# A fixed TensorE order for the recurrence stage of a decoder block, and 64-wide blocks for one level of its triangular inverse

## The chip, the core and the metric

The kernel runs on one core of a Trainium2 chip. A core has a matrix engine (TensorE, PE in the profile, with its weight loads shown apart as PEld), a vector engine (VectorE, DVE), a scalar engine (ScalarE, ACT), GpSimd (POOL) and SyncE (SP), which here issues nearly all transfers. Each engine executes its own instructions in the order in which the program holds them, and waits on semaphores for the others. Matrix products are accumulated in PSUM, which TensorE writes and VectorE and ScalarE read; everything else lies in SBUF or in device memory.

The metric is the time of one execution in microseconds (us); lower is better.

## The reference, cut to what matters

One block of a decoder, one sequence of 512 tokens, model width 2048, all float32:

```python
h = rmsnorm(x) * (1 + sc1) + sh1                 # sh, sc, gt: six parts of silu(c) @ w_ada + b_ada
p = h @ w_in                                     # r, k, v (1024 each), three low-rank inputs, 1024 for pooling
y_rwkv = rwkv7_mixer(...)                        # 16 heads of width 64
y_pool = pool_mixer(...)                         # causal means over windows 2, 4, 8, 16
x = x + gt1 * (concat(y_rwkv, y_pool) @ w_out)
h = rmsnorm(x) * (1 + sc2) + sh2
x = x + gt2 * conv_ffn(h)                        # up-projection, causal conv, silu gate, down-projection
return rmsnorm(x)

# inside rwkv7_mixer, per head, for each token t:
sa = S @ a_t
S  = S * w_t + outer(sa, b_t) + outer(v_t, k_t)
y_t = S @ r_t
```

The mixer is the part at issue. The kernel computes it in chunks of 64 tokens. Inside a chunk the recurrence asks for the inverse of a 64 x 64 unit triangular matrix for each head and chunk; from chunk to chunk a 64 x 64 state is carried on.

## The kernel before

Large products are made in three matmuls: both operands are split into a high part of the type fp32r and a remainder, and `mm3` (lines 122 to 124) adds high x high, high x low and low x high. "A k-tile" below is one such group of three matmuls, 128 x 128 by 128 x 512. The weights of four k-tiles are loaded, rounded on ScalarE (L115, `whi`) and subtracted on VectorE (L117, `wlo`); three buffers of each exist.

The program has these stages in time: the norm and the first eight column blocks of the input projection (tiles `pf`); the recurrence stage, which this change rewrites; the output projection; the feed-forward part.

The recurrence stage has four kinds of work.

- **The rest of the input projection**: 27 column blocks of 16 k-tiles each, 432 k-tiles in all. `win_pair(p)` makes r, k and v of head pair p, shifts them by a token and spills them to device memory; three pool groups of two blocks each follow.
- **Eight head pairs**, each with three functions. `stage_a` makes decays and keys, the scores `bt` against `ar` (L473, tile `pa`), masks them (L414), and inverts the 16 x 16 diagonal blocks: the blocks go to device memory (L419) and come back in another layout (L423); 28 small VectorE instructions (L431 and L433, between L425 and L434) make the inverse; it goes to device memory again (L439), comes back as `x4l` (L442), and ScalarE copies it to `x4` (L445). `stage_b` makes other scores and transposes, and then two levels of products that widen the inverse from 16 to 32 (L512, L521, L524) and from 32 to 64 (L533 to L539). `stage_c` uses the inverse, runs six dependent steps from chunk to chunk (L588 on TensorE, L589 on VectorE), and normalises and gates the result.
- **Pooling** of four groups (`pool_front` on VectorE, `pool_back` on TensorE).
- **`ada_rest`**: 192 rows of a matrix-vector product, each a transfer of 256 KB (L346) and a VectorE instruction with an accumulator read (L347).

The order of the instructions on every engine is made by a scheduler when the program is built. It models the engines' time, takes what is ready, and prefers what has the higher priority. `hp()` gives the pairs' work a higher priority than the projection and `ada_rest`, so the projection's matmuls fill in wherever a pair waits. The granularity is one matmul. Of the input projection, `win_pair(p + 2)` is written ahead of `stage_a(p + 1)`.

`atile` gives one of two PSUM buffers (`pa`), `mmtile` one of two (`mm`), `btile` a double bank (`pb`, and `py` for the outputs).

Of the kernel before, what the change touches and what calls it, by code (L numbers as in the profile page):

```python
# [57 lines left out]
def block_kernel(ctx, tc, a, out, stop=None, dbg=None):  # L58
# [217 lines left out]
    def pool_front(gi):  # L276
# [19 lines left out]
    def pool_back(gi, zs, pw):  # L296
        for d in range(2):
            ps = atile()
            for i in range(2):
                PE.matmul(ps, pw[:, i, d * P : (d + 1) * P], zs[i], start=i == 0, stop=i == 1)  # L300
            j = gi * 2 + d
            mx = ring("mxp")
            S.activation(mx, ps, AF.Identity, bias=drv[:, 35 + j : 36 + j], scale=col("psc", j))
            if gi:
                nc.sync.dma_start(mixd[8 + j], mx)
            else:
                last_mix.append(split_act(14 + d, mx))

# [13 lines left out]
    def win_tile(fi):  # L322
        ps = mmtile()
        project(ps, a["win1"][fi - 8, :, :], H)
        return ps
# [3 lines left out]
    xy = ra.tile([P, 2, 8, 64], F32, tag="xy", name="xy")  # L329
    G.memset(xy, 0.0)  # L330
    dxz = [tc.dram_tile([32, 2, 32, 32], F32, name=f"dxz{i}") for i in range(2)]
    for i in range(2):
        nc.sync.dma_start(dxz[i][:, :, :, :].rearrange("l w i j -> (l w i j)").rearrange("(p n) -> p n", p=P),
                          xy[:, :, :, 0:32])
# [21 lines left out]
    def r8(t, n=64):  # L356
        return t[:, 0 : 8 * n].rearrange("p (s j) -> p s j", s=8)
# [4 lines left out]
    def stage_a(p, rkv):  # L362
        q = Pair()
# [43 lines left out]
        V.tensor_mul(ch(bt), ch(bt), em[:, :, 1 : L + 1])  # L407

# [3 lines left out]
        scores([pss[h] for h in range(2)], bt, ar)  # L412
# [32 lines left out]
        S.copy(q.x4, x4)  # L445


        k2 = ring("k2")
        S.activation(k2, al, AF.Identity, bias=drv[:, 27 + p : 28 + p], scale=col("ka", p))
        V.tensor_mul(k2, k2, k)  # L450
        kt = q.kt = ra.tile([P, T], F32, tag="kt", name="kt", bufs=2)
        V.tensor_mul(ch(kt), ch(k2), em[:, :, 1 : L + 1])
        V.scalar_tensor_tensor(k2, r, col("rk", p), k2, op0=ALU.mult, op1=ALU.mult)
# [5 lines left out]
        return q  # L459

    def half32(b):
        return slice(32 * (b % 2), 32 * (b % 2) + 32)

    def jl(j):
        return slice(j * L, (j + 1) * L)

    def scores(banks, keys, ar):

        for c in range(NC):
            for e in range(2):  # L470
                for h in range(2):
                    j = 2 * c + e
                    PE.matmul(banks[h][HS[e], c * 2 * L : (c + 1) * 2 * L], keys[HS[h], jl(j)], ar[HS[h], :, j, :],  # L473
                              start=True, stop=True)
# [4 lines left out]
    def to_rows(src, dst, eng):  # L479
# [4 lines left out]
        eng(dst, ps[:, :].rearrange("p (c h d) -> p h c d", c=NC, h=2))  # L484

    def stage_b(p, q):
        sb, x4, ar, bt, kt, v = q.sb, q.x4, q.ar, q.bt, q.kt, q.v
        nt = sb[:, :, 0, :]

        tok = q.tok = ra.tile([P, 2, 8, L], F32, tag="tok", name="tok")  # L490
        rw = q.rw = ra.tile([P, 8, 2, L], F32, tag="rw", name="rw")
        sk = q.sk = ra.tile([P, 8, 2, L], F32, tag="sk", name="sk")
# [4 lines left out]
        to_rows(lambda c: v[:, c * P : (c + 1) * P], by_head(tok[:, 0, :, :]), S.copy)  # L497
        to_rows(lambda c: ar[:, 0, 2 * c : 2 * c + 2, :].rearrange("p e t -> p (e t)"), by_head(rw[:, :, 0, :]), S.copy)
        to_rows(lambda c: bt[:, c * P : (c + 1) * P], by_head(sb[:, :, 2, :]), S.copy)
        to_rows(lambda c: kt[:, c * P : (c + 1) * P], by_head(tok[:, 1, :, :]), S.copy)  # L500
        pl = atile()
        for s in range(8):
            for e in range(2):
                PE.matmul(pl[HS[e], jl(s)], sk[HS[e], s, 0, :], tok[HS[e], 0, s, :], start=True, stop=True)
        S.copy(rw[:, :, 1, :], r8(pl))

        X, Y = x4[:, :, 0, :], x4[:, :, 1, :]
        pt = btile()
        pT, pX = pt[:, 0, :], pt[:, 1, :]
        for s in range(8):  # L510
            for b in range(4):
                PE.matmul(pT[BS[b], s * 32 : s * 32 + 32], nt[BS[b], s, half32(b)], X[BS[b], s, :], start=True, stop=True,  # L512
                          tile_position=(32 * b, 32 * b))
        Tm = ra.tile([P, 8, 32], F32, tag="Tm", name="Tm4")
        V.tensor_mul(Tm, r8(pT, 32), mlev[:, 0:1, 0:32].to_broadcast([P, 8, 32]))
        for w in range(2):
# [758 lines left out]
```

## Time and profile before

| | us |
|---|---|
| three executions: median (lowest to highest) | 2380.74 (2366.47 to 2384.72) |
| the profiled execution | 2386.22 |
| its span, first to last instruction | 2384.5 |
| TensorE busy in the span | 2248.9 |
| VectorE busy | 1623.7 |
| ScalarE busy | 1051.7 |
| mean granted TensorE clock, as a share of full speed | 0.973 |

The profiled execution is 1.7 us longer than its span, and 5.5 us longer than the median of the three. "Busy" of TensorE counts pipelined matmuls to modelled ends, so that it is more than the time between their starts. A row of a group gives source line, engine, operation, output and inputs, sizes and count, then the busy time, the mean time of one in ns, and the idle time of the engine ahead of them with what ended it. A row of the timeline gives start and duration in us. A row of a stretch gives its limits, its length, each engine's busy time with the number of instructions, the granted clock, and the share of time in which the transfer engines were busy.

### The profile page before, as it was taken

Reading aid. Unit: us, or ns where it says so; the run is one execution under the profiler, and the core shown is the slowest. Engines: PE = TensorE matmul, PEld = TensorE weight load, DVE = VectorE, ACT = ScalarE, POOL = GpSimd, SP = SyncE. Lnnn points to the kernel's source line nnn. Section 1 sums busy time; section 2 is a strip of 40 time slices with the busy share of each in tenths; the row PEclk is TensorE's granted clock in tenths of the full one; section 3 lists DMA queues with packets and bytes.
Section 4 is the critical chain, followed back from the end, with each engine's and each line's share of the span. In section 5 each row is a group of like instructions: output and inputs, shape, how many; then the busy total and the mean of one; then the engine's idle time right before and its main releaser. Section 6 shows DMA issues by size and latency. Waiting matters only on the chain.

```text
span 2384.5 us, 44692 instructions
## 1 busy us (share of the span) xinstructions
PE 2248.9 (94%) x18114; PEld 1976.6 (83%) x18114; DVE 1623.7 (68%) x2567; ACT 1051.7 (44%) x1451; POOL 126.1 (5%) x183
## 2 busy tenths in 40 slices
PE   4778888999899999999999999999999999999997
PEld 3656666766666789999999999999999888888897
DVE  7987576777774456688888877777777635353354
ACT  3235243444432335655555555555555522233353
POOL 0000000000000000011010100000000000110000
PEclk9999888999989999999999999999999999999999
DMA  9975555556752666498888887777777767763464
GB/s 360 340 228 163 147 162 156 164 168 189 202 168 80 213 203 200 145 293 231 248 234 241 233 220 196 198 197 198 199 198 194 242 206 266 234 203 118 123 185 160
DMA packets 226241, 482.99 MB, mean 203 GB/s; under 512 B 74545, under 2 KB 79729, under 8 KB 217841
## 3 DMA queue, kind: packets, MB, share of 16 engines
q1 hardware_dynamic: 206114, 413.01, 54.5%
q0 software_dynamic: 18864, 66.07, 13.7%
q8 instruction: 142, 2.33, 0.4%
q10 hardware_dynamic: 1056, 1.05, 0.1%
q14 instruction: 65, 0.53, 0.1%
HBM read 441.50 MB, written 38.54 MB: 201 GB/s over the span
## 4 chain that ended last, share of the span: by engine, by line
PE 50%; issue 8%; DVE 1%; ACT 1%; DMA 0%; POOL 0%; POOLq 0%; DVEq 0%; ACTq 0%
PE b L124 17%; PE b L122 17%; PE b L123 17%; ACT x L796 0%; DMA wrow<-wup 0%; DVE xr L793 0%; DVE ulo L865 0%; ACT t L801 0%; DVE t L905 0%; POOL x L1149 0%; DVE wlo L117 0%; DVE u L894 0%; ACT uhi L863 0%; DVE acc L746 0%; POOLq L1270 0%
## 5 line engine op out<-in xcount | busy, mean ns | idle before, releaser
L124 PE MATMUL b<-t,ulo 128*128 128x256 f32 x1408 | 397.2, 282 | 0.0
L122 PE MATMUL b<-t,uhi 128*128 128x256 f32 x1408 | 396.8, 282 | 0.0
L123 PE MATMUL b<-t,uhi 128*128 128x256 f32 x1408 | 396.7, 282 | 0.0
L115 ACT CAST whi<-wraw 128x512 fp32r<-128x512 f32 x236 | 144.9, 618 | 377.5 <-PE mm L123 241.1
L124 PE MATMUL b<-act,ulo 128*128 128x512 f32 (+1 forms) x880 | 308.0, 350 | 0.0
L123 PE MATMUL b<-act,uhi 128*128 128x512 f32 (+1 forms) x880 | 307.7, 350 | 0.0
L122 PE MATMUL b<-act,uhi 128*128 128x512 f32 (+1 forms) x880 | 307.7, 350 | 0.0
L122 PE MATMUL b<-y,uhi 128*128 128x256 f32 x1056 | 298.4, 283 | 2.2 <-ACT uhi L863 2.2
L124 PE MATMUL b<-y,ulo 128*128 128x256 f32 x1056 | 298.0, 282 | 1.0 <-DVE ulo L865 1.0
L123 PE MATMUL b<-y,uhi 128*128 128x256 f32 x1056 | 297.8, 282 | 0.0
L865 DVE TENSOR_TENSOR ulo<-wd,uhi 128x1024 fp32r<-128x1024 f32 (+1 forms) x120 | 136.1, 1135 | 212.0 <-ACT uhi L863 207.2
L122 PEld LDWEIGHTS b<-t,uhi 128*128 128x128 f32 x1408 | 266.9, 190 | 0.0
L124 PEld LDWEIGHTS b<-t,ulo 128*128 128x128 f32 x1408 | 266.9, 190 | 0.0
L123 PEld LDWEIGHTS b<-t,uhi 128*128 128x128 f32 x1408 | 266.8, 190 | 0.0
L863 ACT CAST uhi<-wquart 128x1024 fp32r<-128x1024 f32 x156 | 163.8, 1050 | 203.7 <-PE b L123 174.7
L863 ACT CAST uhi<-wd 128x1024 fp32r<-128x1024 f32 (+1 forms) x120 | 117.3, 978 | 286.8 <-PE b L123 286.7
L865 DVE TENSOR_TENSOR ulo<-wquart,uhi 128x1024 fp32r<-128x1024 f32 x156 | 190.7, 1223 | 72.3 <-ACT uhi L863 71.8
L117 DVE TENSOR_TENSOR wlo<-wraw,whi 128x512 fp32r<-128x512 f32 x236 | 161.0, 687 | 108.6 <-ACT whi L115 100.8
L863 ACT CAST uhi<-r 128x1024 fp32r<-128x1024 f32 x132 | 138.6, 1050 | 163.6 <-PE b L123 163.6
L865 DVE TENSOR_TENSOR ulo<-r,uhi 128x1024 fp32r<-128x1024 f32 x132 | 161.2, 1221 | 62.2 <-ACT uhi L863 62.1
L122 PE MATMUL mm<-ah,whi 128*128 128x512 f32 x464 | 196.9, 424 | 6.2 <-ACT upad L267 5.5
L122 PEld LDWEIGHTS b<-y,uhi 128*128 128x128 f32 x1056 | 200.3, 190 | 2.9 <-ACT uhi L863 2.8
(301 smaller groups left out, 4575.6 us busy)
## 6 DMA issues: line engine op xcount, KB each, us to landing
wquart<-wup SPq DMA_DIRECT2D x176, 512.0 KB, 4.8
wa<-ada SPq DMA_DIRECT2D x48, 1024.0 KB, 6.0
war<-ada SPq DMA_DIRECT2D x192, 256.0 KB, 3.5
wd<-wdn SPq DMA_DIRECT2D x80, 512.0 KB, 4.0
wraw<-win SPq DMA_DIRECT2D x140, 256.0 KB, 4.0
wraw<-wout SPq DMA_DIRECT2D x96, 256.0 KB, 3.4
wquart<-wup POOLq DMA_DIRECT2D x44, 512.0 KB, 7.5
r<-wup SPq DMA_DIRECT2D x44, 512.0 KB, 4.5
```

The costliest lines, as they stand in the source:

```text
L115: S.copy(hi, raw)
L117: eng.tensor_tensor(lo, raw, hi[:, :].bitcast(F32), op=ALU.subtract)
L122: PE.matmul(ps, wh, xh, start=start, stop=False, skip_group_check=more)
L123: PE.matmul(ps, wh, xl, start=False, stop=False, skip_group_check=more)
L124: return PE.matmul(ps, wl, xh, start=False, stop=stop, skip_group_check=more)
L863: S.copy(hi[:, 0:n], src)
L865: lo_of[0] = V.tensor_tensor(lo[:, 0:n], src, hi[:, 0:n].bitcast(F32), op=ALU.subtract)
```

## The change

The order on TensorE is no longer the scheduler's within the recurrence stage: the block `tc.manual_schedule` keeps TensorE's instructions in the order in which the program writes them. The other engines are still ordered by the scheduler. A loop, `recurrence`, writes the work. It holds three chains: `b` (the former `stage_b` and `stage_c` of a pair in one generator), `a` (`stage_a`) and `p` (pooling). Each generator yields two estimates after a step, the TensorE time of the step and the gap until its next step can run, and the loop keeps a clock of its own from them. Where a chain is ready by that clock its next step is written (b ahead of a ahead of p); otherwise one k-tile of the projection, counted as 0.69, and after every second k-tile one row of `ada_rest`. For the inverse, `stage_a` notes a time 27.0 after its scores, and `stage_b` puts its first product with the inverse at that time.

The 16 to 32 level works on 64-wide blocks: `x4` is now 128 x (8, 2, 64) with zeros outside the 32-wide blocks, each product is 16 matmuls of 64 x 64 where it was 32 of 32 x 32, and one VectorE addition replaces four. The copy on ScalarE (now L483) is twice as wide. In `stage_a` the instructions of `k2` and `kt` now stand ahead of the small VectorE instructions. The last products of a pair's outputs stand together after the chunk steps, and the normalisation uses the banks of `py` in place of `pa`. New line numbers: scores L381, mask L447, small instructions L464 to L473, store L478, load L480, first product with the inverse L530, the other products of the two levels L542, L550 and L555, chunk steps L601.

```diff
+    def win_units(fi, ps):
+        src = a["win1"][fi - 8, :, :]
+        for k0 in range(0, KT, WC // P):
+            wh, wl = split_weights(src[:, k0 * P : k0 * P + WC])
+            for kk in range(WC // P):
...
+                mm3(ps, wh[:, sl], wl[:, sl], *H[k], start=k == 0, stop=k == KT - 1)
+                yield
...
-    xy = ra.tile([P, 2, 8, 64], F32, tag="xy", name="xy")
-    G.memset(xy, 0.0)
+    x4w = ra.tile([P, 8, 2, 64], F32, tag="x4", name="x4w")
+    G.memset(x4w, 0.0)
...
@@ stage_a @@
+        sq = ring("sq")
+        S.activation(sq, k, AF.Square, scale=col("kk", p))
+        yield 0.0, 4.0
...
         V.tensor_mul(fdec[:, 0 : NL - 1, :], ep[:, 0 : NL - 1, L : L + 1], em[:, 1:NL, 0:1])
-        sq = ring("sq")
-        S.activation(sq, k, AF.Square, scale=col("kk", p))
+        yield 1.4, 2.0
...
         V.tensor_mul(ch(bt), ch(bt), em[:, :, 1 : L + 1])
+        yield 0.9, 13.0
...
             nc.sync.dma_start(nl[32 * e : 32 * e + 32, :, :], dn[0:32, es, es])
+        k2 = ring("k2")
+        S.activation(k2, al, AF.Identity, bias=drv[:, 27 + p : 28 + p], scale=col("ka", p))
+        V.tensor_mul(k2, k2, k)
+        kt = q.kt = ra.tile([P, T], F32, tag="kt", name="kt", bufs=2)
+        V.tensor_mul(ch(kt), ch(k2), em[:, :, 1 : L + 1])
+        V.scalar_tensor_tensor(k2, r, col("rk", p), k2, op0=ALU.mult, op1=ALU.mult)
...
-        x4 = ra.tile([P, 8, 2, 32], F32, tag="x4", name="x4l")
         for b in range(4):
-            nc.sync.dma_start(x4[BS[b], :, :, :], dx[8 * b : 8 * b + 8, :, :, :].rearrange("s w i j -> i s w j"))
-        q.x4 = ra.tile([P, 8, 2, 32], F32, tag="x4c", name="x4")
-        S.copy(q.x4, x4)
+            nc.sync.dma_start(x4w[BS[b], :, :, half32(b)],
+                              dx[8 * b : 8 * b + 8, :, :, :].rearrange("s w i j -> i s w j"))
+        x4 = q.x4 = ra.tile([P, 8, 2, 64], F32, tag="x4c", name="x4")
+        S.copy(x4, x4w)
+        q.inverted = clock[0] + 27.0
+        yield 1.4, 6.0
...
@@ stage_b @@
+        yield 0.9, max(1.5, q.inverted - clock[0] - 0.9)
...
-        for s in range(8):
-            for b in range(4):
-                PE.matmul(pT[BS[b], s * 32 : s * 32 + 32], nt[BS[b], s, half32(b)], X[BS[b], s, :], start=True, stop=True,
-                          tile_position=(32 * b, 32 * b))
+        for s, e in diag:
+            PE.matmul(pT[HS[e], jl(s)], nt[HS[e], s, :], X[HS[e], s, :], start=True, stop=True)
...
         for w in range(2):
-            for s in range(8):
-                o = 256 * w + s * 32
-                for b in range(4):
-                    l, r_ = (Y, Tm) if w == 0 else (Tm, Y)
-                    PE.matmul(pX[BS[b], o : o + 32], l[BS[b], s, :], r_[BS[b], s, :], start=True, stop=True,
-                              tile_position=(32 * b, 32 * b))
-        for b in range(4):
-            V.tensor_add(xy[BS[b], :, :, half32(b)], x4[BS[b]].rearrange("p s w j -> p w s j"),
-                         pX[BS[b], :].rearrange("p (w s j) -> p w s j", w=2, s=8))
+            for s, e in diag:
+                l, r_ = (Y, Tm) if w == 0 else (Tm, Y)
+                PE.matmul(pX[HS[e], w, jl(s)], l[HS[e], s, :], r_[HS[e], s, :], start=True, stop=True)
+        V.tensor_add(x4, x4, pX[:, :, :].rearrange("p w (s j) -> p s w j", s=8))
+        yield 2.1, 2.3
...
         for j in range(1, NL - 1):
             o = pg[:, j % 2, jl(j // 2)]
             PE.matmul(o, gd[:, j, :], hs[:, j - 1, :], start=True, stop=True)
             V.scalar_tensor_tensor(hs[:, j, :], o, fdec[:, j, :], hs[:, j, :], op0=ALU.mult, op1=ALU.add)
+            yield 0.25, 1.1
...
-        pyc = atile()
+        pyc = py[:, 0, :]
...
-    pool_back(3, pool_front(3), load_pw(3))
-    with hp():
-        q = start_pair(0)
-        stage_b(0, q)
-    win_pair(1)
-    for p in range(NP):
-        if p + 1 < NP:
-            if p + 2 < NP:
-                win_pair(p + 2)
+    def recurrence():
+        units, n, adas = projection(), 0, 0
+        live = {"b": None, "a": None, "p": pool_group(3, load_pw(3), upad)}
+        ready = {"b": 0.0, "a": 0.0, "p": 0.0}
...
+        while True:
+            if live["a"] is None and na < NP and na in made and (na < 2 or hasattr(qs[na - 2], "left")):
+                live["a"], ready["a"] = stage_a(na, qs[na]), clock[0]
+            if live["b"] is None and nb < na:
+                live["b"], ready["b"] = stage_b(nb, qs[nb]), clock[0]
...
+            for c in "bap":
+                if live[c] is not None and ready[c] <= clock[0]:
+                    break
+            else:
+                if more:
+                    more = next(units, 1) is None
+                    if more:
+                        clock[0] += 0.69
+                        n += 1
+                        if n % 2 == 0:
+                            m = min(192, adas + 1)
+                            ada_rest(adas, m)
+                            adas = m
+                    continue
...
             with hp():
-                qn = start_pair(p + 1)
-        with hp():
-            stage_c(p, q)
-            if p + 1 < NP:
-                stage_b(p + 1, qn)
-                q = qn
-        ada_rest(min(28 * p, 192), min(28 * p + 28, 192))
+                step = next(live[c], None)
...
+                clock[0] += step[0]
+                ready[c] = clock[0] + step[1]
+
+    with tc.manual_schedule(engines={mybir.EngineType.PE}):
+        recurrence()
```

More of the change, by code (lines that the diff above doesn't have):

```diff
@@ L458, in stage_a, with to_rows @@
         q.v = v
[L459 to L474, printed above, removed]
+        yield 0.9, 0.0
     def by_head(t):
         return t.rearrange("p (h c) d -> p h c d", h=2)
-    def to_rows(src, dst, eng):
+    def to_rows(src, dst):
         ps = atile()
@@ L501, in stage_b @@
         pl = atile()
-        for s in range(8):
-            for e in range(2):
-                PE.matmul(pl[HS[e], jl(s)], sk[HS[e], s, 0, :], tok[HS[e], 0, s, :], start=True, stop=True)
+        for s, e in diag:
+            PE.matmul(pl[HS[e], jl(s)], sk[HS[e], s, 0, :], tok[HS[e], 0, s, :], start=True, stop=True)
+        Tm = ra.tile([P, 8, 64], F32, tag="Tm", name="Tm4")
+        V.tensor_mul(Tm, r8(pT), mlev[:, 0:1, :].to_broadcast([P, 8, 64]))
         S.copy(rw[:, :, 1, :], r8(pl))
-        X, Y = x4[:, :, 0, :], x4[:, :, 1, :]
@@ L529, in stage_b @@
+        V.tensor_add(x4, x4, pX[:, :, :].rearrange("p w (s j) -> p s w j", s=8))
+        yield 2.1, 2.3
         pt = btile()
         pT, pY = pt[:, 0, :], pt[:, 1, :]
-        for s in range(8):
-            for e in range(2):
-                PE.matmul(pT[HS[e], jl(s)], nt[HS[e], s, :], X[HS[e], s, :], start=True, stop=True)
+        for s, e in diag:
+            PE.matmul(pT[HS[e], jl(s)], nt[HS[e], s, :], X[HS[e], s, :], start=True, stop=True)
         Tm = ra.tile([P, 8, 64], F32, tag="Tm", name="Tm")
@@ new lines, in win_pools @@
+    def win_pools():
+        for n, gi in enumerate((1, 2, 0)):
+            pw = load_pw(gi)
+            upad = []
+            for i in range(2):
+                ps = mmtile()
+                yield from win_units(29 + 2 * n + i, ps)
+                u = ring16("upad")
+                V.memset(u[:, 0:16], 0.0)
+                S.copy(u[:, 16:], ps)
+                upad.append(u)
+            if gi:
+                pools.append(pool_group(gi, pw, upad))
+            else:
+                pools.append((upad, pw))
@@ L698, in block_kernel @@
     with tc.issue_after(last.ins):
-        pool_back(0, zs, pw)
+        for _ in pool_back(0, zs, pw):
+            pass
     pss += [mmtile(), mmtile(), atile(), atile()]
```

178 lines of the change are left out of this document (98 added, 80 removed).

## The prediction

> **What bounds the kernel now.** I began with the stretches of the span, cut at the last `pf` matmul and at the first matmul of the output projection, because only what lies between is rewritten.
>
> ```profile
> 153.90:794.90 641.00, 579.53 (x6507) 421.57 (x6506) 440.94 (x1129) 257.44 (x367) 0.00 (x0) 0.93 0.58 162
> 794.90:2384.50 1589.60, 1567.35 (x11217) 1476.90 (x11215) 1049.96 (x1245) 745.91 (x1011) 123.40 (x172) 0.99 0.71 207
> ```
>
> The recurrence stage takes 641.0 us. TensorE is busy for 579.5 of them, at a mean clock of 0.93. At full clock its work would be 0.93 x 579.5 = 539 us. The other 102 us are waits (61) and slow clock (41). So the most that a better order could gain is about 100 us, and TensorE is the engine to watch: VectorE has 441 us of work. Of the rows that follow the stretch's length, the busy times are those of TensorE, weight loads, VectorE, ScalarE and GpSimd, then come the clock, the transfers' share and GB/s.
>
> Next, the view of waits for TensorE in this stage. Its longest rows:
>
> ```profile
> PE py L592 <- DVE ar L583: 10.0, 7, 3.5
> PE pb L521 <- issue: 8.0, 4, 2.3
> ```
>
> They are many and short. The first product with the inverse, L512, is in no row of that view, although its input goes through device memory twice. The order puts enough other work in front of it. How much, the stretches from the end of a pair's scores to the end of the copy of its inverse (L445) tell:
>
> ```profile
> 195.70:239.50 43.80, 39.35 (x220) 28.73 (x213) 33.30 (x97) 21.38 (x31) 0.00 (x0) 0.92 0.58 150
> 219.70:254.90 35.20, 31.48 (x312) 24.45 (x314) 24.28 (x75) 7.37 (x12) 0.00 (x0) 0.86 0.52 118
> 392.30:442.40 50.10, 46.58 (x377) 33.07 (x367) 34.81 (x102) 19.21 (x28) 0.00 (x0) 0.86 0.63 164
> 598.80:648.10 49.30, 45.08 (x386) 31.99 (x380) 36.86 (x107) 20.57 (x30) 0.00 (x0) 0.97 0.70 188
> sum 376.80, PE 345.07 PEld 250.10 DVE 268.21 ACT 142.42 POOL 0.00; mean PE 43.13 PEld 31.26 DVE 33.53 ACT 17.80 POOL 0.00
> ```
>
> These are pairs 0, 1, 3 and 6, and the sum over all eight: 47.1 us from scores to inverse in the mean, filled with 43.1 us of TensorE. I take this latency apart, since the new order must cover it too.
>
> ```profile
> 208.63 0.41 DVE L425 TENSOR_TENSOR xyl<-nl,lanei 64x256 f32<-64x256 f32 x1
> 230.49 0.38 DVE L434 COPY xyl<-xyl 64x256 f32<-64x256 f32 x1
> 238.87 0.62 ACT L445 COPY x<-x4l 128x512 f32<-128x512 f32 x1 [0.41 <-DMA x4l<-dxz]
> ...
> 237.05 0.41 DVE L425 TENSOR_TENSOR xyl<-nl,lanei 64x256 f32<-64x256 f32 x1
> 244.35 0.37 DVE L434 COPY xyl<-xyl 64x256 f32<-64x256 f32 x1
> 254.23 0.62 ACT L445 COPY x<-x4l 128x512 f32<-128x512 f32 x1 [0.72 <-DMA x4l<-dxz]
> ...
> 408.79 0.41 DVE L425 TENSOR_TENSOR xyl<-nl,lanei 64x256 f32<-64x256 f32 x1
> 427.45 0.38 DVE L434 COPY xyl<-xyl 64x256 f32<-64x256 f32 x1
> 441.83 0.62 ACT L445 COPY x<-x4l 128x512 f32<-128x512 f32 x1
> 442.56 0.75 PE L512 MATMUL pb<-x,sb 32*32 32x32 f32 x64
> 443.24 0.50 PE L124 MATMUL mm<-ah,wlo 128*128 128x512 f32 x1
> ...
> 613.16 0.41 DVE L425 TENSOR_TENSOR xyl<-nl,lanei 64x256 f32<-64x256 f32 x1
> 632.83 0.38 DVE L434 COPY xyl<-xyl 64x256 f32<-64x256 f32 x1
> 647.48 0.61 ACT L445 COPY x<-x4l 128x512 f32<-128x512 f32 x1
> ```
>
> For pairs 0, 1, 3, 6: from the scores' end to L425 (mask, store, load) 12.9, 17.3, 16.5, 14.4 us; from L425 to L434's end (the small VectorE instructions) 22.2, 7.7, 19.0, 20.0; from there to L445 (store, load) 8.0, 9.5, 14.0, 14.3. The two passages through memory cost 20.9 to 30.5 us together. The VectorE part varies with what stands between its 28 small instructions. Those are 0.19 us each, and their neighbours are these:
>
> ```profile
> L347 DVE SCALAR_TENSOR_TENSOR war<-war,cq 128x512 f32<-128x512 f32 x192 | 129.4, 682 | 43.5 <-DMA war<-ada 40.5 <-DMA cq<-cact 2.5
> L117 DVE TENSOR_TENSOR wlo<-wraw,whi 128x512 fp32r<-128x512 f32 x109 | 74.2, 685 | 43.9 <-ACT whi L115 36.9 <-PE mm L124 2.6 <-issue 2.3
> L236 DVE SCALAR_TENSOR_TENSOR spill<-mm,vec,spill 128x511 f32<-128x511 f32 x21 | 15.6, 743 | 4.6 <-ACT spill L235 4.6
> L347 DVE DVE_READ_ACCUMULATOR war<-war,cq 128x1 f32 x192 | 15.3, 80 | 0.0
> L495 DVE TENSOR_TENSOR sk<-pb,masks 128x1024 f32<-128x1024 f32 x8 | 9.8, 1220 | 5.8 <-PE pb L473 5.8
> L524 DVE TENSOR_TENSOR xy<-x,pb 32x512 f32<-32x512 f32 x32 | 21.9, 683 | 13.7 <-PE pb L521 13.3
> ```
>
> Pair 1 has one neighbour and takes 7.7; pair 3 has sixteen, eight of them L347 at 0.76, and takes 19.0. 7.7 plus the neighbours' durations gives the part within about a microsecond.
>
> **The change, part by part.** *Prices on TensorE*, start to start:
>
> ```profile
> 290.09 1.12 PE L611 MATMUL pa<-xg,lw 128*128 128x512 f32 x2 [0.87 <-ACT rs L605]
> 291.05 1.02 PE L612 MATMUL pa<-xg,lw 128*128 128x512 f32 x2
> ...
> 296.00 0.60 PE L483 MATMUL pa<-cmat,kt 128*128 128x128 f32 x4
> 296.54 0.33 PE L521 MATMUL pb<-Tm,x 32*32 32x32 f32 x16
> 296.84 1.15 PE L504 MATMUL pa<-tok,sk 64*64 64x64 f32 x32
> 297.92 1.12 PE L371 MATMUL pa<-xwa,lw 64*128 64x512 f32 x2
> ...
> 505.05 0.39 PE L122 MATMUL mm<-ah,whi 128*128 128x512 f32 x1
> 507.77 0.39 PE L122 MATMUL mm<-ah,whi 128*128 128x512 f32 x1
> ```
>
> A 512-wide float32 product costs 0.96, a batch of four transposes 0.5, sixteen 64-wide matmuls 1.08. Twelve k-tile matmuls lie between the last two rows: 0.227 each, 0.68 a k-tile. A return from a chain's batch to k-tiles costs about 0.2 more (the 0.50 us row at 443.24 against 0.39).
>
> *The wider level.* L512 costs 0.68 (442.56 to 443.24) and L521 two such products; sixteen 64-wide matmuls cost 1.08. Per pair 3 x (1.08 - 0.68) = 1.2 us more, 9.6 in all. The Trainium skill, "TensorEngine Tiling (Array Packing)", Overview, speaks against this edit more strongly: the array makes 16 independent tiles of 32 x 32 and only four of 64 x 64. By a quarter of the price for the narrow form the loss would be 3 x 0.81 x 8 = 19 us; the rows here show 0.68 against 1.08, far from a quarter. On VectorE one wide addition (1.22, as L495) replaces four (2.74): 12 us less in all, 1.5 less on each pair's chain. The order puts two to four k-tiles after those products, which cover either, so I count nothing for it; uncovered, it would be a gain of at most 12.
>
> *The order itself.* In its built form TensorE has 139 runs of k-tiles where there were 147: 8 x 0.2 = 1.6 us less. The work becomes 539 + 9.6 - 1.6 = 547. What decides is how much of it stands between a pair's scores and L530, the first product with the inverse. Counted in the built order, and priced as above (chunk steps 0.4, the closing output products 0.9, both estimates from the 64-wide price):
>
> ```
> pair                            0     1     2     3     4     5     6     7    sum
> k-tiles between                32    26    23    26    24    26    23    26
> TensorE work between, us     26.4  31.3  27.8  26.4  29.7  26.4  27.8  26.4  222.1
> VectorE neighbours             15    16    20    14    10     4     7     9
> of these rows of ada_rest      10    10    11     9     3     0     0     0
> VectorE part, us             18.8  20.0  22.8  18.0  15.4  11.0  13.1  13.4  132.5
> ```
>
> Pair 3 as the example: 26 x 0.68 + five 512-wide products x 0.96 + scores 1.08 + four transposes x 0.5 + four returns x 0.2 = 26.4. Its VectorE part: 7.7 + nine L347 x 0.76 + four L117 x 0.69 + one L236 at 0.74 = 18.0.
>
> So 222 us of TensorE work have to cover eight latencies. The VectorE part is 132.5. The copy is twice as wide; a row of the page bounds it:
>
> ```profile
> L863 ACT CAST uhi<-r 128x1024 fp32r<-128x1024 f32 x132 | 138.6, 1050 | 163.6 <-PE b L123 163.6
> ```
>
> I take 1.05. The two passages are then 21.9 (pair 0) to 31.6 (pair 3) a pair, 27.8 in the mean of the four; the worst pieces together, 17.3 + 14.3 and the copy, make 32.6. I take the mean for pairs 0 to 4 and pair 0's value for 5 to 7, where no `ada_rest` loads are left in the order: 5 x 27.8 + 3 x 21.9 + 132.5 = 337 us. Ends: 8 x 21.9 + 132.5 = 308 and 8 x 32.6 + 132.5 = 393.
>
> TensorE is in order: at L530 it stops until the copy is done, and with it every k-tile behind it. The stop is 337 - 222 = 115 us, 14 a pair.
>
> *The rest of the stage.* Outside these stretches the new order holds 547 - 222 = 325 us of work. Before, 641 - 377 = 264 us held 539 - 0.90 x 345 = 228 (0.90 being the mean clock of the four stretches shown), so 36 us went to waits and slow clock, 16%. Now two k-tiles stand in each gap between chunk steps, which is more than before, so I take 20, between 0 and 52.
>
> *Moved at no cost.* `k2` and `kt` are three VectorE instructions of L117's size and run while the first load is under way; without that cover they lengthen a latency by 3 x 0.69 = 2.1. The normalisation in `py` waits for nothing new: the bank's next writer comes half a pair later. `ada_rest` is spread out; its 192 loads pass between the inverse's transfers on SP as they did, which the passages' prices contain.
>
> **Sum:** 337 + 325 + 20 = 682 us against 641: 41 us more. The profiled execution took 2386.2 with 2384.5 in its span; it becomes 2427. The median of the runs is 5.5 below the profiled one, so I forecast **2422**.
>
> The Trainium skill, "TensorE: Matmul & The Clock Gate", Why this matters for your kernels, asks for no idle gaps over about 3 us, after which the clock falls to half. The trace agrees that the clock falls here (0.86 in pair 3's stretch). By its window of 3.4 us each stop would cost 1.7 more, 14 in all: an estimate, 696 in place of 682.
>
> **The rivals.** *The order covers the inverse (faster).* If the small instructions ran as in pair 1 (7.7) with pair 0's passages, a latency would be 29.6: 8 x 29.6 + 345 = 582, 59 less, 2322. For it: pair 1 did run so. Against: the built VectorE order holds four to twenty neighbours in every pair. The point from which it decides: the stage is equal at a mean latency of (641 - 345) / 8 = 37 us, and over 1% faster below 34.
>
> *No change.* Pair 0's passages everywhere with the built VectorE order: 308 + 345 = 653, 12 more, 2393. For it: later pairs have a quieter queue. Against: of four pairs only one was so short.
>
> *The old latency stays.* 377 us of the old sum, plus 3 for the copy: 380 + 345 = 725, 84 more, 2465. For it: VectorE works as much as before. Against: ten neighbours and fewer in the later pairs.
>
> That the order isn't kept can be ruled out: the built program has it.
>
> **How the numbers follow.** Forecast 0.48, no change 0.24, old latency 0.14, faster 0.14. About 1% is what a measurement of this kernel can tell from no change. Over 1% faster: 0.14 and a little of the second case, 0.15; within 1%: 0.24; slower: 0.61. The range goes from 2350, half-way into the faster case, to 2490, the long end of the passages (393 + 345 = 738, 97 more) with some of the 52.
>
> **What would show it.** Right: TensorE waits for the copy to `x4` (L483) about eight times, 8 to 20 us each, some 115 in all; 13 to 23 us lie between L464 and L473 in pairs 0 to 4, less after; the rewritten stage takes about 680; L542 takes 2.2 a pair. Wrong: no long wait at L530 and a stage under 620; or the loss elsewhere, as in waits between chunk steps or VectorE standing behind `ada_rest`'s loads.

## The result, and the profile after

| | before | after |
|---|---|---|
| median of the runs compared, us | 2373.93 | 2441.62 |
| lowest to highest | 2366.47 to 2384.72 | 2439.10 to 2447.94 |
| profiled execution / its span | 2386.22 / 2384.5 | 2447.94 / 2446.0 |

The change makes the kernel slower: 1.0286 times the time before, with a 95% interval of 1.0232 to 1.0339. The forecast was 2422, in a range of 2350 to 2490; the measured time lies in it, 20 us above the forecast. (The 2380.74 from which the forecast started is the median of three executions; the 2373.93 has a fourth, of 2367.12.)

The stretches of the changed kernel, cut at the same two places as in the prediction:

```profile
155.20:858.40 703.20, 549.60 (x5738) 418.20 (x5737) 437.48 (x1105) 255.08 (x362) 0.00 (x0) 0.90 0.52 147
858.40:2446.00 1587.60, 1565.93 (x11217) 1475.74 (x11215) 1050.34 (x1245) 746.31 (x1011) 123.59 (x172) 0.99 0.70 207
```

The recurrence stage grew from 641.0 to 703.2 us and everything behind it kept its length (1589.6 and 1587.6). TensorE's busy time in the stage fell from 579.5 to 549.6, so the waits grew from 61.5 to 153.6. Which waits, the view of TensorE's waits in this stage says (us in total, how often, the longest):

```profile
PE pa L530 <- ACT x L483: 84.7, 8, 16.8
PE pb L601 <- DVE rw L602: 16.5, 7, 4.0
PE pa L300 <- DVE inv L432: 15.3, 1, 15.3
PE py L628 <- DVE rs L623: 8.9, 7, 2.0
...
PE py L593 <- issue: 5.2, 3, 3.2
PE pb L562 <- DVE sb L556: 4.6, 2, 3.4
```

The first row is the stop of the prediction: TensorE waits at the first product with the inverse for ScalarE's copy, eight times, 10.6 us in the mean. Before, this product was in no row. The other rows stand outside the inverses. The stretches from a pair's scores to the end of the copy (pairs 0, 2, 5 and 7, and the sum of all eight; columns as in the prediction):

```profile
204.30:245.80 41.50, 26.06 (x146) 20.64 (x146) 26.48 (x83) 10.06 (x16) 0.00 (x0) 0.86 0.83 230
...
363.60:409.40 45.80, 27.47 (x163) 20.22 (x163) 28.38 (x91) 13.76 (x20) 0.00 (x0) 0.80 0.73 207
...
620.60:652.60 32.00, 25.50 (x138) 18.77 (x136) 16.22 (x45) 13.68 (x20) 0.00 (x0) 0.97 0.53 118
...
763.10:795.20 32.10, 25.48 (x136) 18.71 (x136) 16.55 (x48) 12.46 (x18) 0.00 (x0) 0.98 0.38 83
sum 313.10, PE 213.20 PEld 156.94 DVE 185.66 ACT 104.97 POOL 0.00; mean PE 26.65 PEld 19.62 DVE 23.21 ACT 13.12 POOL 0.00
```

The eight latencies sum to 313 us (377 before) and hold 213 us of TensorE work (345 before). A pair has 25.5 to 28.5 us of work in front of its inverse, and the inverse takes 32 to 46. One stop, pair 2's, on the timeline of TensorE:

```profile
392.20 0.39 PE L124 MATMUL mm<-ah,wlo 128*128 128x512 f32 x1
409.44 1.97 PE L530 MATMUL pa<-x,sb 64*64 64x64 f32 x32 [16.85 <-ACT x L483]
```

Ahead of it stands the last k-tile of this pair's 23, behind it the first product; the k-tiles that TensorE could have done meanwhile are queued behind L530. The clock around this stop:

```profile
394.00:409.40 15.40, 0.00 (x0) 0.00 (x0) 8.92 (x30) 1.56 (x2) 0.00 (x0) 0.53 0.82 227
409.40:415.30 5.90, 5.86 (x69) 5.31 (x70) 4.22 (x13) 0.59 (x1) 0.00 (x0) 0.50 0.59 190
415.30:430.00 14.70, 14.70 (x197) 11.76 (x195) 11.03 (x25) 2.45 (x4) 0.00 (x0) 1.00 0.77 236
```

It falls to half within the stop and stays there for 5.9 us of the work that follows, which costs some 3 us more. All eight stops ended at half clock.

The fall of the busy time has a source of its own. With the stage cut at every change of the granted clock, 87 of the 579.5 us and 72 of the 549.6 us were busy at half clock. Counted as half, these leave an estimate of the work at full clock: 536 us before and 514 after, although the wider level has come in. Matmuls of a pair that the scheduler had spread out now run in one batch. The group with the largest difference among these, before and after (the same 224 matmuls; a part of it is the clock):

```profile
L592 PE MATMUL py<-ar,rw 64*64 64x64 f32 x224 | 24.6, 295 | 10.0 <-DVE ar L583 10.0
...
L606 PE MATMUL py<-ar,rw 64*64 64x64 f32 x224 | 8.2, 222 | 0.0
```

So the change saves TensorE work and then loses more than that in waits.

### The profile page after: what moved, and what is told of

Same layout as the page of the kernel before. It is cut to its first block, busy times and chain, and to the rows that moved or that the text cites. A ratio compares the mean times of both kernels' runs of the same rounds, so it can differ in the third digit from the quotient of the medians.

```text
span 2446.0 us, 43166 instructions
## 1 busy us (share of the span) xinstructions
PE 2217.8 (91%) x17346; PEld 1972.2 (81%) x17346; DVE 1620.6 (66%) x2543; ACT 1049.9 (43%) x1447; POOL 126.3 (5%) x183
## 4 chain that ended last, share of the span: by engine, by line
PE 48%; issue 8%; DVE 1%; DMA 1%; ACT 0%; POOL 0%; POOLq 0%; DVEq 0%; ACTq 0%
PE b L124 16%; PE b L123 16%; PE b L122 16%; DMA wrow<-wup 1%; DVE ulo L923 0%; DVE xr L851 0%; ACT x L854 0%; DVE t L977 0%; POOL x L1207 0%; ACT t L859 0%; ACT uhi L921 0%; DVE u L952 0%; DVE wlo L117 0%; DVE t L963 0%; DVE t L969 0%
## 5 line engine op out<-in xcount | busy, mean ns | idle before, releaser
L117 DVE TENSOR_TENSOR wlo<-wraw,whi 128x512 fp32r<-128x512 f32 x236 | 161.4, 688 | 109.0 <-ACT whi L115 106.7
L122 PE MATMUL mm<-ah,whi 128*128 128x512 f32 x464 | 208.4, 449 | 5.5 <-ACT upad L267 5.5
L923 DVE TENSOR_TENSOR ulo<-r,uhi 128x1024 fp32r<-128x1024 f32 x132 | 161.3, 1222 | 61.5 <-ACT uhi L921 61.3
```

Of the source, the lines that this page charges most:

```text
L117: eng.tensor_tensor(lo, raw, hi[:, :].bitcast(F32), op=ALU.subtract)
L122: PE.matmul(ps, wh, xh, start=start, stop=False, skip_group_check=more)
L923: lo_of[0] = V.tensor_tensor(lo[:, 0:n], src, hi[:, 0:n].bitcast(F32), op=ALU.subtract)
```

## The experiments

All are edits of the changed kernel. "Stop" is the row of the wait at the first product with the inverse; "other waits" are the stage less TensorE's busy time in it, less the stop. Ratios are to the kernel before, with 95% intervals.

| run | time | ratio | stage | busy | stop | other waits |
|---|---|---|---|---|---|---|
| changed kernel | 2441.6 | 1.0286 (1.0232 to 1.0339) | 703.2 | 549.6 | 84.7 | 69 |
| gap 34 | 2385.8 | 1.0038 (1.0017 to 1.0059) | 642.9 | 543.0 | 25.2 | 75 |
| 32-wide level | 2436.1 | 1.0266 (1.0223 to 1.0309) | 696.6 | 546.0 | 76.1 | 74 |
| constant in place of the inverse | 2363.5 | 0.9955 (0.9931 to 0.9979) | 610.4 | 530.5 | 0 | 80 |
| rows left out | 2354.1 | 0.9893 (0.9860 to 0.9926) | 610.8 | 535.6 | 35.1 | 40 |
| late pooling | 2422.0 | 1.0168 (1.0134 to 1.0202) | 683.2 | 550.7 | 66.7 | 66 |
| gap 34, late pooling | 2382.6 | 1.0018 (0.9997 to 1.0039) | 638.8 | 543.3 | 25.9 | 70 |
| rows tied, late pooling | 2402.9 | 1.0109 (1.0082 to 1.0136) | 660.8 | 546.6 | 41.2 | 73 |
| rows tied, late pooling, gap 34 | 2362.6 | 0.9933 (0.9907 to 0.9960) | 598.3 | 531.0 | 0.6 | 67 |
| the same, three rows for two | 2375.3 | 0.9994 (0.9976 to 1.0012) | 632.0 | 541.0 | 6.8 | 84 |
| scheduler's order | 2366.3 | 0.9968 (0.9943 to 0.9993) | 625.2 | 587.0 | 1.9 | 36 |
| scheduler's order, 32-wide level | 2424.9 | 1.0193 (1.0155 to 1.0231) | 667.5 | 608.5 | 10.4 | 49 |
| scheduler's order, rows tied | 2407.7 | 1.0129 (1.0093 to 1.0166) | 672.6 | 621.2 | 0 | 51 |

The theory was that of the prediction: a stop is a pair's latency less the TensorE work that the order puts in front of it, and the stops are the loss.

### More work in front of the inverse

```diff
-        q.inverted = clock[0] + 27.0
+        q.inverted = clock[0] + 34.0
```

> One number changes: the first product with the inverse is placed 34.0 after the scores on the loop's own clock, not 27.0. Counted in the built order, 296 us of TensorE work now stand between the scores and that product in the eight pairs, not 222. The stops there came to 85 us in the changed kernel. Theory (the stop is latency less work in front of it): the small VectorE instructions get 117 neighbours in place of 95, 22 x 0.75 = 16 us more latency, so the stops fall to 85 - 74 + 16 = 27 us (a little more, since no pair's stop goes below nothing), the stage by about 55 us, the time to 2385 (2370 to 2405). Rival (the stage is bounded by something else, and the k-tiles moved ahead are only missed elsewhere): the stops move to chunk steps and pooling, the time stays at 2425 to 2445.

Its stage, in the rows of the stretches, its sum over the eight stretches from scores to copy, and its longest wait:

```profile
155.90:798.80 642.90, 542.99 (x5738) 412.02 (x5738) 434.16 (x1105) 253.74 (x363) 0.00 (x0) 0.94 0.57 161
```

```profile
sum 337.40, PE 279.14 PEld 209.83 DVE 223.99 ACT 127.18 POOL 0.00; mean PE 34.89 PEld 26.23 DVE 28.00 ACT 15.90 POOL 0.00
```

```profile
PE pa L530 <- ACT x L483: 25.2, 4, 8.5
```

66 us more TensorE work lie in front of the inverses (279 against 213); the latencies grew by 24, of which 11 between the small VectorE instructions and 14 ahead of the masks, where other work on VectorE now stands; the stops fell from 84.7 to 25.2, and the stage by 60. In the eight stretches TensorE's idle time fell by only 42 (from 100 to 58), because matmuls of the neighbouring pair, with waits of their own, now lie in them too. The time is the expected one, 2386. Seven us more in one estimate take back 56 of the 68 us of loss.

### No wait for the inverse

```diff
-        S.copy(x4, x4w)
+        S.copy(x4, ident[:, None, :].to_broadcast([P, 8, P]).rearrange("p s (w j) -> p s w j", w=2))
```

> The inverse of the 16-wide blocks is still computed and carried through device memory, but the copy on ScalarE fills x4 from a constant, so that the first product with the inverse waits for no transfer; its value is left out of the outputs. Theory (the stop is the whole of the loss): the 85 us at that product go, the stage shortens by 85 or, with the clock that falls to half after the stops, by up to 110: 2330 to 2357. Rival (TensorE is held back by something as late, VectorE or the weights' splitting, in the same stretches): waits of another name take over half of the 85, 2395 to 2420.

The stage and the longest waits:

```profile
154.00:764.40 610.40, 530.50 (x5736) 401.32 (x5737) 432.89 (x1105) 253.49 (x361) 0.00 (x0) 0.96 0.60 169
```

```profile
PE pb L601 <- DVE rw L602: 17.9, 9, 3.6
PE pa L300 <- DVE inv L432: 14.7, 1, 14.7
PE py L628 <- DVE rs L623: 9.7, 7, 2.1
```

The stage is 93 us shorter than in the changed kernel, inside the 85 to 110 expected; the median, 2363, is 6 above the expected range, while the profiled run (span 2351.2) was one of its short ones. The 93 consist of 74 us of waits (153.6 to 79.9: of the 84.7, 11 return elsewhere) and 19 us of busy time for the same matmuls, which is the clock: 0.96 in place of 0.90, while the work at full clock is the same (516 and 514). The two profiled executions are the shortest of ten here and the longest of four in the changed kernel, 95 us apart where the medians are 78 apart, so a part of the 93, and of the 19, can be the spread between executions. By the medians the stops cost 78 us, which is more than the whole loss of 68 against before; the slow clock behind them is at most about a fifth of what they cost.

### Where the latency comes from

The rows of `ada_rest` are left out, except one:

```diff
-        units, n, adas = projection(), 0, 0
+        units, n, adas = projection(), 0, 191
```

> 191 of the 192 rows of ada_rest (transfer and VectorE instruction) are left out, and the sums that they make are left out of the outputs; order and estimates on TensorE are those of the changed kernel. The small VectorE instructions then have 43 neighbours in place of 95. Theory (latency is fixed passages plus 7.7 plus neighbours): 52 x 0.76 = 40 us less latency and passages as in the quieter pairs 5 to 7, some 10 less, so the latencies sum to about 265 (313 in the changed kernel), the stops fall from 85 to about 35, the time to 2390 (2370 to 2400; less where waits on VectorE elsewhere in the stage shrink too). Rival (the passages through device memory are the latency, and the rows only fill VectorE's idle time): 2425 to 2442.

Stage, sum of the stretches from scores to copy, longest wait:

```profile
155.30:766.10 610.80, 535.59 (x5738) 408.86 (x5738) 323.67 (x722) 254.77 (x363) 0.00 (x0) 0.95 0.33 86
```

```profile
sum 251.20, PE 208.56 PEld 155.18 DVE 131.69 ACT 104.92 POOL 0.00; mean PE 26.07 PEld 19.40 DVE 16.46 ACT 13.12 POOL 0.00
```

```profile
PE pa L531 <- ACT x L484: 35.1, 8, 7.1
```

With the same order on TensorE the latencies fall from 313 to 251 (265 expected) and the stops from 84.7 to 35.1 (35 expected). The VectorE parts sum to 89 us (122 in the changed kernel) and the masks, passages and copies to 162 (191): the rows make the latency long from both sides, among the small instructions and in the masks and passages around them. (This run leaves out the rows' transfers with their instructions, so it doesn't tell the two apart.) The time, 2354, is 36 below the expected 2390 and 16 below the end of the range, because the other waits fell too, from 69 to 40, and the busy time by 14: the chunk steps and the pooling wait for VectorE, and the rows stand in their way as well. The expectation named this as possible and gave no number for it.

### The wide level

The 16 to 32 level and its copy go back to 32-wide blocks in the same order (L530 and L542 as 32 matmuls of 32 x 32, four additions for one). The table of that level's mask stays that of 64-wide blocks, so the products hold other numbers.

> The 16 to 32 level alone goes back to 32-wide blocks, in the same fixed order. Theory (prices of the traces): three batches a pair at 0.68 in place of 1.08 us, 9.6 us less TensorE work, all of it behind the stop at the inverse; the copy is 0.43 shorter, 3.4 in all; four additions of 0.68 in place of one of 1.22 cost up to 12 where the k-tiles behind the products don't cover them. So 0 to 13 us less, 2435. Rival by the quarter price of 32-wide tiles: 19 + 3 us less, 2420. Rival (the wide level is the loss): 40 less or more, 2400.

```profile
155.20:851.80 696.60, 546.03 (x6504) 411.08 (x6505) 448.25 (x1129) 251.28 (x362) 0.00 (x0) 0.90 0.52 149
```

5.5 us less than the changed kernel, inside the 0 to 13 expected, and nothing like the 19 + 3 of a quarter price. The work at full clock is 503 us against 514, near the 9.6 that the prediction counted. Of the sixteen and four tiles behind the quarter price both forms use only those on the diagonal, four of 32 and two of 64, so that count didn't apply to them. Against the kernel before the narrow level is nearly as slow as the wide one: the wide level isn't the loss.

### The pooling group

```diff
-        ready = {"b": 0.0, "a": 0.0, "p": 0.0}
+        ready = {"b": 0.0, "a": 0.0, "p": 40.0}
```

The third wait of the changed kernel, 15.3 us at L300, comes once, at the start. TensorE and VectorE there:

```profile
172.26 0.39 PE L124 MATMUL mm<-ah,wlo 128*128 128x512 f32 x1
187.96 6.39 PE L300 MATMUL pa<-z,pw 128*128 128x512 f32 x8 [15.30 <-DVE inv L432]
```

```profile
172.40 0.69 DVE L354 SCALAR_TENSOR_TENSOR war<-war,cq 128x512 f32<-128x512 f32 x1
...
186.60 0.69 DVE L354 SCALAR_TENSOR_TENSOR war<-war,cq 128x512 f32<-128x512 f32 x1 [0.26 <-DMA war<-ada]
187.21 0.69 DVE L432 TENSOR_SCALAR inv<-pa 128x512 f32<-128x512 f32 x1
```

Eleven rows of `ada_rest` run on VectorE between the two matmuls, among the pooling's own instructions, and L432 ahead of L300 reads a `pa` buffer. Moving the group alone, and then with the gap of 34:

> The first pooling group's chain may start 40 us later on the loop's own clock; nothing else changes, and the built order still has 228 us of TensorE work in front of the inverses (222 in the changed kernel). Theory (TensorE stood 15.3 us at that group's first product because its VectorE inputs were late): this wait is gone, 15 us less, 2427 (2420 to 2432). Rival (the group's product only happened to be next; whatever stands there meets the same VectorE queue): the wait returns under another name, 2436 to 2445.

> The gap of 34.0 for the inverse and the pooling group 40 us later, together; 299 us of TensorE work stand in front of the inverses. Theory (the two stops are separate and in series on TensorE): 2386 less 15 for the pooling, 2370 (2362 to 2378), about the kernel before or a little under it. Rival (they hide each other): 2380 to 2390.

The longest waits of the first, in its view of waits:

```profile
PE pa L530 <- ACT x L483: 66.7, 8, 15.3
PE pb L601 <- DVE rw L602: 17.9, 6, 5.6
PE py L628 <- DVE rs L623: 11.9, 7, 3.3
PE mm L124 <- DVE wlo L117: 6.7, 2, 4.6
```

The first came to 2422, 20 less than the changed kernel, about as expected, but not for the reason expected: L300 is gone from the view, yet the waits outside the inverses fell only from 69 to 66, because k-tiles now wait for their weights' splitting (L117) and the gates (L628) wait longer. The 18 us came off the stops: 9 at pair 1, whose inverse now has 34 us of TensorE work in front of it (28 before), and 6 at pair 0. With the gap of 34, where the stops are small, the same edit brought 3 us, 2383, as the rival had it: in both runs, most of what waited for VectorE at the start waits for it elsewhere.

### The rows outside the inverses

The rows are written only outside a pair's inverse, there one after every k-tile (one after every second before), and queued on VectorE behind the last copy (L473) of the latest inverse. The pooling group stays 40 us late:

```diff
-                        if n % 2 == 0:
+                        if not busy():
                             m = min(192, adas + 1)
-                            ada_rest(adas, m)
+                            if inverse[0] is None:
+                                ada_rest(adas, m)
+                            else:
+                                with tc.issue_after(inverse[0].ins):
+                                    ada_rest(adas, m)
```

> The 192 rows of ada_rest stay, but are written only outside a pair's inverse and queued on VectorE behind the last copy of the pair's small instructions; the pooling group is 40 us late as before, the gap for the inverse is 27.0. The small instructions have 49 neighbours in place of 95. Theory (the rows among the small instructions make the latency long): as in the run without rows the stops at the first product with the inverse fall to about 35 us from the 67 of the run with the later pooling group, its 2422 becomes 2390 (2380 to 2400). Rival (the rows only change places, and the chunk steps or the masks wait for them now): 2410 to 2425.

> The same with the gap of 34.0: 36 neighbours, about 300 us of TensorE work in front of the inverses, whose latencies should sum to about 265. Theory: the 26 us of stops that were left with this gap go, 2383 becomes 2357 (2345 to 2365), faster than the kernel before. Rival (waits on VectorE at the chunk steps grow by what the stops lose): 2375 to 2385.

With the gap of 27 the stops fell to 41.2 (35 expected), but the matmuls behind the splitting (L117) and the products after the chunks' inverse (L574) waited longer, 14.6 and 12.3: 2403, 13 above the forecast, between theory and rival. With the gap of 34, the stage, the stretch behind it, and the sum of the stretches from scores to copy:

```profile
155.20:753.50 598.30, 530.95 (x5737) 402.71 (x5738) 410.95 (x1012) 250.36 (x360) 0.00 (x0) 0.96 0.53 153
...
753.50:2360.70 1607.20, 1572.81 (x11217) 1478.16 (x11215) 1077.81 (x1338) 745.29 (x1011) 123.38 (x172) 0.99 0.70 212
```

```profile
sum 277.40, PE 260.02 PEld 196.44 DVE 180.98 ACT 111.39 POOL 0.00; mean PE 32.50 PEld 24.55 DVE 22.62 ACT 13.92 POOL 0.00
```

The fixed order now covers the inverse: latencies of 277 with 260 us of work, a single stop of 0.6, and a stage of 598, 43 less than before the change. The VectorE parts sum to 85 us and the masks are done 15 us after the scores in all, where it was 135 and 29 in the run with gap 34 and late pooling, which differs by this edit alone; the passage behind the last copy (L473), where rows now run, grew from 96 to 105. And 45 rows were left for the time behind the stage, where they lengthen it by 20:

```profile
L354 DVE SCALAR_TENSOR_TENSOR war<-war,cq 128x512 f32<-128x512 f32 x45 | 30.4, 690 | 21.0 <-DMA war<-ada 21.0
```

The time is 2362.6, as expected 2345 to 2365, and 0.7% under the kernel before. A further run brings these rows back by writing three for two k-tiles in place of two:

> The kernel with the gap of 34.0, the late pooling group and the tied rows, with three rows of ada_rest for every two k-tiles outside an inverse (two before), so that fewer rows are left for the stage after. Theory: the 45 rows that ran after the recurrence stage made the stage behind it 20 us longer; most of these come back, while pair 0's small instructions get 9 rows more among them (7 us): 2363 - 20 + 7 = 2350 (2342 to 2358). Rival (the rows' VectorE time is paid wherever it stands): 2360 to 2368.

```profile
155.40:787.40 632.00, 541.03 (x5736) 409.09 (x5737) 436.78 (x1105) 251.14 (x360) 0.00 (x0) 0.94 0.56 164
...
787.40:2373.50 1586.10, 1565.09 (x11217) 1475.26 (x11216) 1050.01 (x1245) 746.09 (x1011) 123.55 (x172) 0.99 0.70 208
```

```profile
PE mm L124 <- DVE wlo L117: 16.2, 2, 15.1
PE pb L602 <- DVE rw L603: 14.8, 7, 3.0
```

In the first fence stand the stage and the stretch behind it, in the second the two longest waits. It missed, with 2375 above both the theory (to 2358) and the rival (to 2368): the stretch behind the stage lost its 21 us (1586.1), and the stage gained 34, 10 of it in busy time at a lower clock. The 45 rows cost more in the stage than behind it.

### The scheduler's order

The same loop writes the work, and TensorE is ordered by the scheduler:

```diff
-    with tc.manual_schedule(engines={mybir.EngineType.PE}):
-        recurrence()
+    recurrence()
```

> The loop writes the same chains, k-tiles and rows in the same order, with the wider level, but TensorE is ordered by the scheduler like the other engines. Theory (TensorE standing at the first product with the inverse, with k-tiles behind it, is the loss): the scheduler puts k-tiles there again, no wait over 4 us is left at that product, and the time comes to that of the kernel before plus the wider level, 2374 + 10 = 2385 (2370 to 2400). Rival (the rewritten chains themselves, their buffers and their VectorE order cost the time): 2425 to 2445.

> TensorE ordered by the scheduler and the 16 to 32 level on 32-wide blocks, with the rewritten chains: against the run with the scheduler's order and the wide level (2366.3) it gives the price of the wide level where TensorE rarely stops. The table of that level's mask stays that of 64-wide blocks, so the products hold other numbers. Theory of the prediction (9.6 us more TensorE work in the wide form, the shorter VectorE addition hidden): 2357. Rival (the one addition of 1.22 us in place of four of 0.68 is on the pair's chain and worth more than the matmuls): 2367 to 2378, no better than the kernel before.

> TensorE ordered by the scheduler, the wide level, and the rows outside the inverses (77 neighbours in that built order). Theory: the scheduler's order already has no stop at the inverse (1.9 us), so shorter latencies bring nothing there: 2366, give or take the 10 us that other waits on VectorE move. Rival (the two runs with the scheduler's order, 2366 and 2425, differ by accidents of that order, which any edit stirs): anywhere from 2350 to 2425.

```profile
154.90:780.10 625.20, 587.01 (x5737) 433.62 (x5738) 430.27 (x1105) 248.31 (x357) 0.00 (x0) 0.93 0.57 165
```

```profile
PE pb L601 <- DVE rw L588: 11.7, 7, 2.6
...
PE pa L530 <- ACT x L483: 1.9, 1, 1.9
```

The first run did what the theory asked: almost no stop, 38 us of waits in all, 2366, 4 below the expected range. But the other two have no great stops either and came to 2425 and 2408. Their stages:

```profile
154.90:822.40 667.50, 608.51 (x6504) 442.44 (x6505) 443.78 (x1129) 248.98 (x359) 0.00 (x0) 0.90 0.53 155
```

```profile
155.50:828.10 672.60, 621.20 (x5737) 449.93 (x5738) 434.82 (x1105) 245.87 (x356) 0.00 (x0) 0.89 0.52 154
```

And the two rows of the third with the longest single waits:

```profile
PE pb L556 <- DVE Tm L553: 7.0, 4, 5.2
PE pa L404 <- ACT upad L267: 5.4, 1, 5.4
```

The third does the matmuls of the first with 13 us more of waits and 34 more of busy time, at a clock of 0.89. Cut at the changes of the clock, the work at full clock is 547, 550 and 549 us in the three, while 81, 118 and 145 us of their busy time ran at half clock: much of what sets them apart is the clock, the rest waits. Three builds with the scheduler's order thus differ by 59 us, which the rival of the third had allowed for, so 2366 alone doesn't say what that order is worth, and the price of the wide level can't be read from the second: both its theory (2357) and its rival (2367 to 2378) missed. Why the clock was low there without long stops stays open; no run told it apart. Against the same chains in the scheduler's order, the fixed order saves 547 - 514 = 33 us of TensorE work at full clock; that is its gain, and the stops and waits hide it in the changed kernel.

## Why the forecast held, and where it was off

**The place.** Right: 62.2 us of loss in the rewritten stage, nothing behind it.

**The latency** was put at 337 us and came to 313. The VectorE part was 132.5 by the sum of neighbours and measures 122; the passages with the copy were 27.8 or 21.9 a pair and measure 23.9 in the mean. So 10.5 of the 24 us lie in the VectorE part and 13.6 in the passages, 12 of these in pairs 0 to 4, for which the mean of four old pairs, 27.8, was taken and which came to 25.5. The small instructions took 15 to 22 us in pairs 0 to 4 and 10 to 13 after, as forecast.

**The stop** was put at 115 us. TensorE was idle for 313 - 213 = 100 in these stretches, 84.7 of it at L530, eight times and for the copy, as forecast; each was 6 to 17 us, not 8 to 20. The 222 us of work between scores and L530, counted with prices from the trace, measured 213. L542 takes 2.0 a pair, near the 2.2. The mechanism is shown by two runs that change one thing each: more work in front (stop 25) and shorter latency (stop 35).

**The rest of the stage** is the term that was mis-sized: 325 + 20 = 345 us forecast, 703 - 313 = 390 measured. TensorE was busy for 549.6 - 213.2 = 336 us of it, which is 304 at full clock, so the work of 325 was put 21 too high; waits of 390 - 336 = 54 and 32 of slow clock came where 20 stood for both. The work was too high because the total of 547 took off only 1.6 us for the new order: 547 is what the scheduler's order of these chains has, and the fixed order has 514. The waits were too low because the reason given, that two k-tiles in each gap between chunk steps would hold them down, failed: L601 waited 16.5 us, the gates 8.9, the pooling 15.3. Every run with the fixed order keeps such waits (66 to 84 us beside the stop), except the one without the rows on VectorE (40). The list of wrong signs named waits between chunk steps and VectorE behind the rows; the sum had no term for the pooling.

So 24 us too much for the latency and 45 too little outside it make the 21 us by which the stage missed its 682, and the time its 2422 by 20. The forecast came near partly by luck: the latency was put too high and the rest too low, and within the rest the work was too high and the waits too low.

**The slow clock** was held as 14 us by the rule of the Trainium skill, "TensorE: Matmul & The Clock Gate", Why this matters for your kernels, and not taken into the sum. All eight stops ended at half clock, and the constant in place of the inverse has up to 19 us less busy time, so the trace agrees with the rule and the larger sum of that sentence, 696, was nearer. The stretch of pair 3, which the prediction showed for it, doesn't bear on gaps: its clock was 0.86 without a wait over 1.3 us.

**The wide level**: 9.6 us of TensorE work less up to 12 on VectorE, counted as 9.6; taking it back gave 5.5, and 11 of work at full clock. Right. **`k2` and `kt`** at no cost: right, mask and passage to L464 took 11 to 16 us (12.9 to 17.3 before).

**The rivals.** "Old latency stays" fell: 313, not 377. "No change" had 308 us of latency, close to what came, and a time of 2393 that was wrong because it too had 345 outside. "The order covers the inverse" needed a mean latency under 37; it was 39 in the changed kernel. In the two runs that came under it, 31.4 without the rows and 34.7 with the rows tied and more work in front, the time did fall below that before.

## What to carry to other kernels

Where an in-order engine's order is fixed by estimates, an estimate that is too short costs its shortfall every time it is used, with all ready work queued behind: here 100 us of idle time for 313 us of latency with 213 of work. Before fixing an order, measure the longest latency in it as the program will run, with what else its engines have to do, and put at least that much work in front. Here 7 us more in one number were worth 56 us. The gain of such an order, 33 us of TensorE work here, shows only when the stops are gone. Shorten the latency first by taking bulk work off the engine that carries its chain, and look at where that work goes, because it can cost more in its new place.

## What the runs showed of the hardware

The clock of TensorE fell within a stop of 17 us and was back to full only after 5.9 us of work. In the stage with the scheduler's order and the rows tied it was 0.89 in the mean although TensorE was busy for 621 of 673 us and its longest wait was 5.4: a low clock doesn't need long stops, and what sets it there was not found. The kernel before shows the same: half clock for 13.6 us in pair 3's stretch, with TensorE busy for 13.3 of them and chunk steps and k-tiles in turn.
